# Regrouping wide and narrow matmuls, and one PSUM tile per bank, in the feed-forward part of a decoder layer

## The chip, the core and the metric

The kernel runs on one core of a Trainium2 chip. The metric is the device time in microseconds of one execution, and the number to predict is the median of several runs of the changed kernel. Five engines work side by side, each through its own instruction stream in order: TensorE (PE, with its weight loads as PEld), VectorE (DVE), ScalarE (ACT), GpSimd (POOL, unused here) and SyncE (SP), which issues all loads.

## What is computed

One decoder layer on 256 tokens of width 2048, in float32: two groups of attention heads, an output projection and a gated feed-forward part of inner width 5504. The change lies in the feed-forward part. Cut from the reference:

```python
def conv_ffn(h, w_up, conv_w, conv_b, w_down):
    u = h @ w_up                                   # 2048 -> 2 x 5504
    up = jnp.pad(u, ((0, 0), (CONV_WIDTH - 1, 0), (0, 0)))
    uc = conv_b
    for i in range(CONV_WIDTH):
        uc = uc + up[:, i:i + S] * conv_w[i]
    gate, val = jnp.split(uc, 2, axis=-1)
    return (jax.nn.silu(gate) * val) @ w_down      # 5504 -> 2048
...
h2 = rmsnorm(x, norm2_g[l]) * (1.0 + sc2) + sh2
x = x + g2 * conv_ffn(h2, w_up[l], conv_w[l], conv_b[l], w_down[l])
return rmsnorm(x, final_norm_g)
```

## The kernel before

**Precision.** Every float32 matrix is split into a high part (rounded to the matmul's format) and a low part (the rest): `split` (L142) makes `wh` with a cast on ACT (L145) and `wl` with a subtraction on DVE (L146), 1024 columns at a time, each in a ring of three buffers. A ring slot is refilled when PE has read its last matmul from it. Weights come in loads of 1 MB (2048 columns a partition) into a ring of four `raw` buffers, issued by SP in program order.

**Two ways to multiply.** `trn` (L161) gives three matmuls of 256 columns per 128x128 block of weights: high by high (L163), high by low (L164), low by high (L165). `fold` (L155) gives two: a wide one, `wh` against the 512 columns that hold the high and the low part of the activations side by side (L158), and a narrow one of 256 columns, `wl` against the high part alone (L159). Each matmul loads its own weights. A split of 1024 columns is 8 blocks, called a chunk here: 24 matmuls by `trn`, 16 by `fold`.

**Up projection.** `do_U` (L790) makes the accumulators of one of 43 column tiles f (gate and value) from two loads, i = 0 and 1, and so from four chunks (tiles `wU` f i gv). For f under 8 `trn` is used, and the i = 0 halves of all eight stand ahead of the i = 1 halves, since the second half of the input `h2` is made late; two neighbouring f share one PSUM tile of two banks (tile U0 holds f = 0 and 1). From f = 8 on `fold` is used, and a tile of two banks holds gate and value of one f. After each f its accumulators are drained: for f of 8 and above a copy of the low half on ACT (L836) and an addition on DVE (L837), both 512 wide; then the convolution (L843 on ACT, L847 on DVE), the silu (L849), the product (L853) and the high and low parts of the result (L854, L855) in `aT`.

**Down projection.** The loop at L862 goes through 43 loads of `wD`; 43 blocks make one output tile k, so a chunk of 8 can hold the end of one k and the start of the next. Two neighbouring k share one PSUM tile of two banks (`banks`, L796). When a k is complete, DVE reads it (L875, then L726 in `resid`), ACT squares the result (L731) and scales it (L877).

**What sets the order.** The program is written as one stream; the framework under it works out from the tiles that instructions share which must wait for which, orders each engine's instructions by priority and readiness, and puts in the waits. A PSUM tile is one object to it. Pools give buffers by tag: `s2` (2 KB a partition, four of them) serves the small intermediates of the whole layer: `h` and `g2` of the normalisations, the rotary pieces, the `rl` tiles of the index scores (L549 and on), masks, and `u` and `uc` of the up projection. A table (`PLAN`, L48) and a rate place the `wa` and `wg` loads of the conditioning matrix, with one DVE operation of 2.3 us for each `wa` (L215).

The table of psum pools: stage 3 (up and down) has four buffers of two banks each, eight banks in all.

Of the kernel before, what the change touches and what calls it, by code (L numbers as in the profile page):

```python
# [10 lines left out]
F32 = mybir.dt.float32  # L11
# [3 lines left out]
AF = mybir.ActivationFunctionType  # L15
ALU = mybir.AluOpType
AX = mybir.AxisListType
PSUM = bass.MemoryType.PSUM

P = 128  # L20
D = 2048
S = 256
NT = 2
KT = 16
# [5 lines left out]
FT = 43  # L30
# [8 lines left out]
PB, PN1, PN2, PSG, PDG, PCW, PCB, PC, PGF = 0, 96, 112, 128, 136, 144, 402, 488, 504  # L39
# [15 lines left out]
def layer(ctx: ExitStack, tc: tile.TileContext, a, out):  # L55
    nc = tc.nc
    V, A, T, DMA = nc.vector, nc.scalar, nc.tensor, nc.sync

    cp = ctx.enter_context(tc.tile_pool(name="cp", bufs=1))
    wp = ctx.enter_context(tc.tile_pool(name="wp", bufs=1))  # L60
# [2 lines left out]
        return wp.tile(shape, dt, name=name, tag="b8", bufs=17)  # L63

    def s2(shape, dt, name):
        return wp.tile(shape, dt, name=name, tag="s2", bufs=4)

    def sm(n, name):
        return wp.tile([P, n], F32, name=name, tag="sm", bufs=8)
# [36 lines left out]
    def rb(name):  # L106
        return wp.tile([P, S], F32, name=name, tag="rb", bufs=2)
# [34 lines left out]
    def split(w, off, n, name):  # L142
        wh = wp.tile([P, 1024], F32R, name=name + "h", tag="wh", bufs=3)
        wl = wp.tile([P, 1024], F32R, name=name + "l", tag="wl", bufs=3)
        lo_[1] = A.copy(out=wh[:, 0:n], in_=w[:, off:off + n])  # L145
        lo_[0] = V.tensor_tensor(out=wl[:, 0:n], in0=w[:, off:off + n], in1=wh[:, 0:n].bitcast(F32), op=ALU.subtract)  # L146
        return wh, wl
# [4 lines left out]
        T.matmul(pt, lhsT=xh, rhs=wl, start=False, stop=False)  # L152
        T.matmul(pt, lhsT=xl, rhs=wh, start=False, stop=last)

    def fold(pt, x, wh, wl, first, last):  # L155


        T.matmul(pt, lhsT=wh, rhs=x, start=first, stop=False)  # L158
        T.matmul(pt[:, 1, :], lhsT=wl, rhs=x[:, 0, :], start=False, stop=last)  # L159

    def trn(pt, xh, xl, wh, wl, first, last):  # L161

# [45 lines left out]
    def order(later, earlier):  # L208
        tc.add_manual_dep(later.ins, earlier.ins.name,
                          mybir.DependencyInfo(mybir.DependencyClass.NoSync, mybir.DependencyReason.DATA),  # L210
                          reason="order")
# [512 lines left out]
    def resid(dst, acc, gate, res, sqsum, k, name):  # L724

        resid_i[0] = V.scalar_tensor_tensor(out=dst, in0=acc, scalar=gate, in1=res, op0=ALU.mult, op1=ALU.add)  # L726
        if k == 0:
            A.activation(sqsum, dst, AF.Square)
            return None
        sq = s2([P, S], F32, f"{name}{k}")  # L730
        resid_i[1] = A.activation(sq, dst, AF.Square)  # L731
        if k >= KT - 2:
            return sq
        V.tensor_tensor(out=sqsum, in0=sqsum, in1=sq, op=ALU.add)
# [39 lines left out]


    ctx3 = ExitStack()

    pool3 = ctx3.enter_context(tc.tile_pool(name="psC", bufs=4, space=PSUM))
    psum_pool[0] = (pool3, {"ps": 4})
    ptag[0] = "ps"  # L780

    def banks(name):
        return pool3.tile([P, 2, 2, S], F32, name=name, tag="ps", bufs=4)

    aT = []

    G0 = 8
    uacc = {}

    def do_U(f, i):  # L790

        if i == 0:
            if f >= G0:
                uacc[f] = banks(f"U{f}")
            elif f % 2 == 0:
                t_ = banks(f"U{f}")  # L796
                uacc[f], uacc[f + 1] = t_[:, 0], t_[:, 1]
        w = load(a["wU"][f, i], 2048, f"wU{f}{i}")
        for gv in range(2):
            wh, wl = split(w, gv * 1024, 1024, f"wU{f}{i}{gv}")  # L800
            if (f, i, gv) in ((0, 0, 1), (1, 0, 0)):
                order(lo_[0], resid_i[0])
                if gv == 0:
                    order(lo_[1], resid_i[1])
            for j in range(8):
                k = 8 * i + j
                x = h2[k // 4][:, k % 4, :, :]
                sl = slice(j * P, (j + 1) * P)
                if f >= G0:
                    fold(uacc[f][:, gv], x, wh[:, sl], wl[:, sl], k == 0, k == KT - 1)  # L810
                else:
                    trn(uacc[f][:, gv, :], x[:, 0, :], x[:, 1, :], wh[:, sl], wl[:, sl], k == 0 and gv == 0,
                        k == KT - 1 and gv == 1)

    def eager(n=2):
        for k in range(KT):
# [11 lines left out]
    for f in range(FT):  # L828
        if f >= G0:
            do_U(f, 0)  # L830
        do_U(f, 1)
        acc = uacc.pop(f)
        pump()
        if f >= G0:
            u = s2([P, 2, S], F32, f"u{f}")
            A.copy(out=u, in_=acc[:, :, 1, :])  # L836
            V.tensor_tensor(out=u, in0=acc[:, :, 0, :], in1=u, op=ALU.add)  # L837
        else:
            u = acc
        uc = s2([P, 2, S], F32, f"uc{f}")  # L840
        for gv in range(2):
            i = 2 * f + gv
            A.activation(uc[:, gv, :], u[:, gv, :], AF.Identity, scale=par[:, PCW + 3 * i + 2:PCW + 3 * i + 3],  # L843
                         bias=par[:, PCB + i:PCB + i + 1])
            for sft in (1, 2):
                o = PCW + 3 * i + 2 - sft
                V.scalar_tensor_tensor(out=uc[:, gv, sft:S], in0=u[:, gv, 0:S - sft], scalar=par[:, o:o + 1],  # L847
                                       in1=uc[:, gv, sft:S], op0=ALU.mult, op1=ALU.add)
        last_silu = A.activation(uc[:, 0, :], uc[:, 0, :], AF.Silu)  # L849
        if f % 4 == 0:  # L850
            aT.append(b8([P, 4, 2, S], F32R, f"aT{f}"))
        at = aT[f // 4][:, f % 4, :, :]
        V.tensor_tensor(out=uc[:, 1, :], in0=uc[:, 0, :], in1=uc[:, 1, :], op=ALU.mult)  # L853
        A.copy(out=at[:, 0, :], in_=uc[:, 1, :])  # L854
        V.tensor_tensor(out=at[:, 1, :], in0=uc[:, 1, :], in1=at[:, 0, :].bitcast(F32), op=ALU.subtract)  # L855
# [3 lines left out]
        need(j)  # L859
    V.tensor_tensor(out=mod[:, 80:96], in0=mod[:, 80:96], in1=par[:, PB + 80:PB + 96], op=ALU.add)  # L860
    sq3, last = rb("sq3"), [None, None]
    for q in range(FT):  # L862
        w = load(a["wD"][:, q * 2048:(q + 1) * 2048], 2048, f"wD{q}")
        for p_ in range(2):
            wh, wl = split(w, p_ * 1024, 1024, f"wD{q}{p_}")
            for j in range(8):
                k, f = divmod((2 * q + p_) * 8 + j, FT)
                if f == 0 and k % 2 == 0:
                    acc = banks(f"W{k}")
                fold(acc[:, k % 2], aT[f // 4][:, f % 4, :, :], wh[:, j * P:(j + 1) * P], wl[:, j * P:(j + 1) * P],  # L870
                     f == 0, f == FT - 1)
                if f == FT - 1:
                    xk = x1T[k // 8][:, k % 8, :]
                    g = mod[:, 80 + k:81 + k]
                    V.scalar_tensor_tensor(out=xk, in0=acc[:, k % 2, 0, :], scalar=g, in1=xk, op0=ALU.mult, op1=ALU.add)  # L875
                    last[k % 2] = resid(xk, acc[:, k % 2, 1, :], g, xk, sq3, k, "x2q")
                    A.activation(xk, xk, AF.Copy, scale=par[:, PGF + k:PGF + k + 1])  # L877
    r3 = rms_b([sq3] + last, D, None, "r3", "ps")
    for k, n in ((0, 2), (2, 2), (4, 4), (8, 4), (12, 4)):
        y = x1T[k // 8][:, k % 8:k % 8 + n, :]  # L880
# [72 lines left out]
```

## Time and profile before

| | |
|---|---|
| median of 3 runs | 1251.4 us (1251.29 to 1252.37) |
| the profiled execution's own time | 1258.62 us |
| its span on the core | 1256.8 us |
| PE busy | 1171.3 us (93%) |
| PE weight loads busy | 1016.9 us (81%) |
| DVE busy | 880.5 us (70%) |
| ACT busy | 629.3 us (50%) |
| mean granted TensorE clock | 0.979 |
| DMA | 303.48 MB, mean 241 GB/s |

All times of single instructions come from the one profiled execution. A matmul's recorded duration reaches past the start of the next one, since they are pipelined; what a matmul costs in a stream is therefore read from the distance between starts (its pitch), not from its duration. In the trace's stretches, up runs from about 477 to 988 us (f under 8 until about 595) and down from about 988 to 1243 us.

### The profile page before, as it was taken

How to read it: one execution, taken by the hardware profiler on the slowest of the kernel's cores; microseconds unless marked ns; L12 is line 12 of the kernel's file. 1: busy time of each engine (PE TensorE's matmuls, PEld its weight loads, DVE VectorE, ACT ScalarE, POOL GpSimd, SP SyncE). 2: the span in 40 equal slices, each digit the busy share in tenths (PEclk: the TensorE clock that was granted, in tenths of full speed). 3: DMA queues.
4: the chain of work that ended last, by engine and by line, in shares of the span. 5: the costliest groups of instructions: out<-in, count | busy, mean ns of one | idle time of the engine just before them, and what ended most of it. 6: DMA issues, size and time to landing. Idle time of an engine off the chain costs nothing.

```text
span 1256.8 us, 17813 instructions
## 1 busy us (share of the span) xinstructions
PE 1171.3 (93%) x7120; PEld 1016.9 (81%) x7120; DVE 880.5 (70%) x1232; ACT 629.3 (50%) x969; POOL 0.2 (0%) x4
## 2 busy tenths in 40 slices
PE   4699999899999997988999999999999999999995
PEld 2478987567879997987888888888888888888885
DVE  4877787789667888756789778777777645545443
ACT  3355554466555544454555555555555543443441
POOL 0000000000000000000000000000000000000000
PEclk9799999999999998999999999999999999999998
DMA  8988989667678896844578666666665445455431
GB/s 307 365 332 303 339 331 336 231 252 277 228 293 351 298 330 258 306 165 168 181 250 316 224 226 229 215 241 224 214 225 190 179 172 192 172 175 183 179 135 67
DMA packets 43282, 303.48 MB, mean 241 GB/s; under 512 B 4928, under 2 KB 5440, under 8 KB 7232
## 3 DMA queue, kind: packets, MB, share of 16 engines
q1 hardware_dynamic: 43200, 302.35, 66.0%
q8 instruction: 55, 0.90, 0.3%
q14 instruction: 27, 0.22, 0.0%
HBM read 300.24 MB, written 2.10 MB: 241 GB/s over the span
## 4 chain that ended last, share of the span: by engine, by line
PE 82%; DVE 11%; ACT 3%; DMA 2%; issue 2%; SPq 0%; DVEq 0%; ACTq 0%
PE U L158 20%; PE W L158 13%; PE U L159 10%; PE W L159 6%; DVE wa L215 3%; PE U L165 2%; PE U L164 2%; PE U L163 2%; PE O L165 2%; PE O L163 2%; PE O L164 2%; PE QK L163 2%; PE QK L164 2%; PE QK L165 2%; DMA wa<-wa 2%; PE A L151 2%
## 5 line engine op out<-in xcount | busy, mean ns | idle before, releaser
L215 DVE SCALAR_TENSOR_TENSOR wa<-wa,scb 128x2048 f32<-128x2048 f32 x76 | 173.5, 2285 | 6.9 <-DMA wa<-wa 6.6
L847 DVE SCALAR_TENSOR_TENSOR uc<-u,par,uc 128x254 f32<-128x254 f32 (+1 forms) x140 | 58.2, 478 | 0.0
L843 ACT ACTIVATE uc<-u,par 128x256 f32<-128x256 f32 x70 | 38.2, 593 | 0.8 <-DVE u L837 0.8
L854 ACT CAST aT<-uc 128x256 fp32r<-128x256 f32 x43 | 17.4, 404 | 28.8 <-DVE uc L853 28.7
L313 ACT ACTIVATE amul<-mod,b,par 128x1 f32<-128x1 f32 x32 | 12.0, 385 | 32.2 <-DVE wa L215 32.2
L192 PE MATMUL ap<-wg,csil 128*32 128x512 f32 x160 | 26.4, 679 | 0.3 <-DVE mod L201 0.3
L855 DVE TENSOR_TENSOR aT<-uc,aT 128x256 fp32r<-128x256 f32 x43 | 18.2, 422 | 10.0 <-ACT aT L854 9.9
L837 DVE TENSOR_TENSOR u<-U,u 128x512 f32<-128x512 f32 x35 | 23.9, 684 | 0.0
L316 ACT ACTIVATE mod<-mod,par 128x1 f32<-128x1 f32 x32 | 8.6, 302 | 27.5 <-DVE wa L215 26.6
L836 ACT COPY u<-U 128x512 f32<-128x512 f32 x35 | 20.3, 580 | 0.0
L853 DVE TENSOR_TENSOR uc<-uc 128x256 f32<-128x256 f32 x43 | 18.1, 420 | 1.5 <-ACT uc L849 0.7
L849 ACT ACTIVATE uc<-uc 128x256 f32<-128x256 f32 x43 | 17.7, 411 | 1.5 <-DVE uc L847 1.5
L731 ACT ACTIVATE x2q<-x1T 128x256 f32<-128x256 f32 x15 | 6.2, 415 | 21.3 <-DVE x1T L726 21.2
L875 DVE SCALAR_TENSOR_TENSOR x1T<-W,mod,x1T 128x256 f32<-128x256 f32 x16 | 7.7, 481 | 12.0 <-PE W L159 12.0
L847 DVE SCALAR_TENSOR_TENSOR uc<-U,par,uc 128x255 f32<-128x255 f32 (+1 forms) x32 | 14.5, 477 | 1.4 <-ACT uc L843 1.2
L192 PEld LDWEIGHTS ap<-wg,csil 128*32 128x32 f32 x160 | 4.7, 120 | 10.0 <-issue 8.2
L843 ACT ACTIVATE uc<-U,par 128x256 f32<-128x256 f32 x16 | 9.0, 561 | 7.5 <-DVE uc L847 7.5
L676 ACT ACTIVATE sbt<-sbt 128x384 f32<-128x384 f32 x8 | 4.2, 524 | 14.8 <-DVE sbt L675 14.8
L562 DVE SCALAR_TENSOR_TENSOR scw<-rl,wix,scw 128x128 f32<-128x128 f32 (+1 forms) x28 | 10.4, 409 | 0.0
L545 PE MATMUL rel<-ws,qixT 64*128 64x128 f32 (+1 forms) x64 | 8.5, 345 | 2.0 <-ACT rl L550 2.0
L273 PE MATMUL cb<-ident,csil 128*128 128x128 f32 x16 | 3.6, 422 | 7.1 <-DMA ident<-ident 7.1
L197 ACT COPY rw<-ap 128x512 f32<-128x512 f32 x5 | 2.9, 586 | 14.0 <-PE ap L192 13.3
(2810 smaller groups left out, 4600.7 us busy)
## 6 DMA issues: line engine op xcount, KB each, us to landing
wU<-wU SPq DMA_DIRECT2D x86, 1024.0 KB, 4.8
wa<-wa SPq DMA_DIRECT2D x76, 1024.0 KB, 5.4
wD<-wD SPq DMA_DIRECT2D x43, 1024.0 KB, 4.6
wg<-wg SPq DMA_DIRECT2D x20, 1024.0 KB, 6.2
wA<-wA SPq DMA_DIRECT2D x16, 1024.0 KB, 6.4
wQK<-wQK SPq DMA_DIRECT2D x16, 1024.0 KB, 6.9
wO<-wO SPq DMA_DIRECT2D x16, 1024.0 KB, 6.9
xT<-xT SPq DMA_DIRECT2D x4, 512.0 KB, 5.9
```

What stands on the lines that cost most here:

```text
L151: T.matmul(pt, lhsT=xh, rhs=wh, start=first, stop=False)
L158: T.matmul(pt, lhsT=wh, rhs=x, start=first, stop=False)
L159: T.matmul(pt[:, 1, :], lhsT=wl, rhs=x[:, 0, :], start=False, stop=last)
L163: T.matmul(pt, lhsT=wh, rhs=xh, start=first, stop=False)
L164: T.matmul(pt, lhsT=wh, rhs=xl, start=False, stop=False)
L165: T.matmul(pt, lhsT=wl, rhs=xh, start=False, stop=last)
L192: T.matmul(pt[32 * j:32 * j + 32, :], lhsT=csil[:, k:k + 1].to_broadcast([P, 32]), rhs=w[:, j * 512:(j + 1) * 512], start=q == 0, stop=q == 3)
L215: i = V.scalar_tensor_tensor(out=w, in0=w, scalar=1.0, in1=scb, op0=ALU.mult, op1=ALU.mult, accum_out=mod[:, j:j + 1])
L836: A.copy(out=u, in_=acc[:, :, 1, :])
L837: V.tensor_tensor(out=u, in0=acc[:, :, 0, :], in1=u, op=ALU.add)
L843: A.activation(uc[:, gv, :], u[:, gv, :], AF.Identity, scale=par[:, PCW + 3 * i + 2:PCW + 3 * i + 3], bias=par[:, PCB + i:PCB + i + 1])
L847: V.scalar_tensor_tensor(out=uc[:, gv, sft:S], in0=u[:, gv, 0:S - sft], scalar=par[:, o:o + 1], in1=uc[:, gv, sft:S], op0=ALU.mult, op1=AL ...
```

## The change

Three edits, all in one diff:

1. `fold` takes the eight steps of a chunk and issues the eight wide matmuls first, then the eight narrow ones. Both call sites collect the steps and call it once a chunk.
2. Up and down take one PSUM tile per bank: eight buffers of one bank in place of four of two. In up each f under 8 has a tile of its own, and from f = 8 on gate and value have one each; their drain becomes two copies and two additions of 256 columns in place of one each of 512. In down each k has its own tile, and the reading of a finished k is written behind the whole chunk.
3. The ring `s2` has three buffers in place of four, and `u` moves out of it to a ring `u2` of two.

```diff
     def s2(shape, dt, name):
-        return wp.tile(shape, dt, name=name, tag="s2", bufs=4)
+        return wp.tile(shape, dt, name=name, tag="s2", bufs=3)
...
-    def fold(pt, x, wh, wl, first, last):
-        T.matmul(pt, lhsT=wh, rhs=x, start=first, stop=False)
-        T.matmul(pt[:, 1, :], lhsT=wl, rhs=x[:, 0, :], start=False, stop=last)
+    def fold(steps):
+        for pt, x, wh, _, first, _ in steps:
+            T.matmul(pt, lhsT=wh, rhs=x, start=first, stop=False)
+        for pt, x, _, wl, _, last in steps:
+            T.matmul(pt[:, 1, :], lhsT=wl, rhs=x[:, 0, :], start=False, stop=last)
...
-    pool3 = ctx3.enter_context(tc.tile_pool(name="psC", bufs=4, space=PSUM))
-    psum_pool[0] = (pool3, {"ps": 4})
+    pool3 = ctx3.enter_context(tc.tile_pool(name="psC", bufs=8, space=PSUM))
+    psum_pool[0] = (pool3, {"ps": 8})
...
-    def banks(name):
-        return pool3.tile([P, 2, 2, S], F32, name=name, tag="ps", bufs=4)
+    def bank(name):
+        return pool3.tile([P, 2, S], F32, name=name, tag="ps", bufs=8)
...
         if i == 0:
-            if f >= G0:
-                uacc[f] = banks(f"U{f}")
-            elif f % 2 == 0:
-                t_ = banks(f"U{f}")
-                uacc[f], uacc[f + 1] = t_[:, 0], t_[:, 1]
+            uacc[f] = [bank(f"U{f}{gv}") for gv in range(2)] if f >= G0 else bank(f"U{f}")
...
         if f >= G0:
-            u = s2([P, 2, S], F32, f"u{f}")
-            A.copy(out=u, in_=acc[:, :, 1, :])
-            V.tensor_tensor(out=u, in0=acc[:, :, 0, :], in1=u, op=ALU.add)
+            u = wp.tile([P, 2, S], F32, name=f"u{f}", tag="u2", bufs=2)
+            for gv in range(2):
+                A.copy(out=u[:, gv, :], in_=acc[gv][:, 1, :])
+                V.tensor_tensor(out=u[:, gv, :], in0=acc[gv][:, 0, :], in1=u[:, gv, :], op=ALU.add)
...
+            steps, done = [], None
             for j in range(8):
                 k, f = divmod((2 * q + p_) * 8 + j, FT)
-                if f == 0 and k % 2 == 0:
-                    acc = banks(f"W{k}")
-                fold(acc[:, k % 2], aT[f // 4][:, f % 4, :, :], wh[:, j * P:(j + 1) * P], wl[:, j * P:(j + 1) * P],
-                     f == 0, f == FT - 1)
+                if f == 0:
+                    wacc[k] = bank(f"W{k}")
+                steps.append((wacc[k], aT[f // 4][:, f % 4, :, :], wh[:, j * P:(j + 1) * P], wl[:, j * P:(j + 1) * P],
+                              f == 0, f == FT - 1))
                 if f == FT - 1:
-                    xk = x1T[k // 8][:, k % 8, :]
...
+                    done = k
+            fold(steps)
+            if done is not None:
+                k = done
+                acc = wacc.pop(k)
+                xk = x1T[k // 8][:, k % 8, :]
...
```

The order of instructions changes beyond what the diff says, at three places. In the rows below (those of the changed kernel have its own line numbers) a tile's name carries its buffer number behind an underscore, `x3` is a repetition, and the engines named in brackets are those that the instruction waits for.

**PE, down projection, where k = 0 ends and k = 1 begins (chunk wD21).** Before:

```order
L158 MATMUL W0_8976<-aT40_8765,wD21h_9077 128x512
L159 MATMUL W0_8976<-aT40_8765,wD21l_9078 128x256
L158 MATMUL W0_8976<-aT0_4957,wD21h_9077 128x512 [waits DVE_49]
L159 MATMUL W0_8976<-aT0_4957,wD21l_9078 128x256
L158 MATMUL W0_8976<-aT0_4957,wD21h_9077 128x512
```

With the change:

```order
L160 MATMUL W0_9085<-aT40_8868,wD21h_9186 128x512 [waits DVE_49]
L160 MATMUL W1_9190<-aT0_4961,wD21h_9186 128x512 [waits PE_49]
L160 MATMUL W1_9190<-aT0_4961,wD21h_9186 128x512 x3
L160 MATMUL W1_9190<-aT4_5238,wD21h_9186 128x512
L162 MATMUL W0_9085<-aT40_8868,wD21l_9187 128x256 [waits DVE_49]
L162 MATMUL W0_9085<-aT40_8868,wD21l_9187 128x256 x2
L162 MATMUL W1_9190<-aT0_4961,wD21l_9187 128x256 x4
L162 MATMUL W1_9190<-aT4_5238,wD21l_9187 128x256
```

The first matmul of k = 1 (on aT0) waited for DVE, because it wrote the tile W0 that DVE was to read for k = 0; now it writes a tile W1 of its own and waits for no other engine. The wait for DVE in the first row of the second piece is for the last column tile of aT40, and that in the fifth for wD21l.

**PE, up projection, behind the last chunk of f = 0.** Before:

```order
L163 MATMUL U0_4354<-h23_4301,wU011h_4921 128x256
L164 MATMUL U0_4354<-h23_4301,wU011h_4921 128x256
L165 MATMUL U0_4354<-h23_4301,wU011l_4922 128x256
L163 MATMUL U2_4471<-h22_4300,wU210h_5032 128x256 [waits Activation_49]
L164 MATMUL U2_4471<-h22_4300,wU210h_5032 128x256
L165 MATMUL U2_4471<-h22_4300,wU210l_5033 128x256 [waits DVE_49]
```

With the change:

```order
L166 MATMUL U0_4354<-h23_4301,wU011h_4925 128x256
L167 MATMUL U0_4354<-h23_4301,wU011h_4925 128x256
L168 MATMUL U0_4354<-h23_4301,wU011l_4926 128x256
L166 MATMUL U1_4413<-h22_4300,wU110h_4967 128x256 [waits Activation_49]
L167 MATMUL U1_4413<-h22_4300,wU110h_4967 128x256
L168 MATMUL U1_4413<-h22_4300,wU110l_4968 128x256 [waits DVE_49]
```

Before, the chunks ran wU011, wU210, wU110, wU111, wU211, wU410, wU310, wU311, wU411, wU610, wU510, wU511, wU611, wU800, wU710, wU711: an even f pushed ahead of the odd one that shares a tile with the f being drained. Now they run in rising order, wU011, wU110, wU111, wU210 and on. ACT and DVE make the splits in rising order in both kernels. At the start of up, the first chunks of f = 0 and f = 1 (wU000 and wU100) are now interleaved, where wU000 and wU001 ran through before wU100.

**DVE, index scores of the sparse attention.** `scw` are the score sums and the top-64 search (m815 to m817 its late steps), `rl` the rectified products, V1040l a split of the value projection that PE uses as a filler. Before:

```order
L568 MAX m815_2038<-scw_131 128x8 [waits DVE_49]
L295 TENSOR_TENSOR qx1v_2068<-qds_196,scw_131 128x8x16
L569 MATCH_REPLACE scw_131<-m815_2038,scw_131 128x256 [waits DVE_49]
L296 TENSOR_TENSOR qds_196<-qx1u_2067,qx1v_2068 128x8x32 [waits DVE_49]
L568 MAX m816_2041<-scw_131 128x8 [waits DVE_49]
L146 TENSOR_TENSOR V1040l_2340<-V10w4_2331,V1040h_2339 128x1024 [waits DMAHW0_49]
```

With the change:

```order
L565 SCALAR_TENSOR_TENSOR scw_131<-rl001_1911,wix_1861,scw_131 128x128 [waits DVE_49]
L565 SCALAR_TENSOR_TENSOR scw_131<-rl010_1927,wix_1861,scw_131 128x128 [waits DVE_49,Activation_49]
L146 TENSOR_TENSOR V1040l_2340<-V10w4_2331,V1040h_2339 128x1024 [waits DMAHW0_49]
L565 SCALAR_TENSOR_TENSOR scw_131<-rl010_1927,wix_1861,scw_131 128x128 [waits DVE_49]
L565 SCALAR_TENSOR_TENSOR scw_131<-rl011_1933,wix_1861,scw_131 128x128 [waits Activation_49]
```

V1040l moved from the end of the search to the first group of scores, and with it the other splits of the value and query-key projections come earlier on ACT and DVE. PE then has V1040 and V1042 matmuls ahead of the transposes kdsp and qdsp, and takes the sparse attention's and the stick-breaking heads' own matmuls somewhat later among the same fillers. SP's order of loads is the same in both kernels.

## Rows read from the trace of the kernel before

**Rows 1.** The page, busy time, share of the span and instructions of engines

```profile
PE 1171.3 (93%) x7120; PEld 1016.9 (81%) x7120; DVE 880.5 (70%) x1232; ACT 629.3 (50%) x969; POOL 0.2 (0%) x4
```

**Rows 2.** Busy by stretch: us, PE, PEld, DVE, ACT, POOL, clock, DMA share, GB/s

```profile
225.00:400.00 175.00, 160.93 (x1062) 128.25 (x1055) 133.73 (x256) 102.14 (x218) 0.00 (x0) 0.98 0.73 271
536.00:600.00 64.00, 54.50 (x391) 51.56 (x391) 41.04 (x65) 31.79 (x49) 0.00 (x0) 0.95 0.46 162
600.00:1000.00 400.00, 399.73 (x2263) 346.30 (x2263) 306.73 (x422) 223.97 (x319) 0.00 (x0) 1.00 0.63 225
1000.00:1245.00 245.00, 232.19 (x1316) 200.64 (x1314) 116.95 (x125) 97.18 (x111) 0.00 (x0) 1.00 0.45 159
```

**Rows 3.** PE's waits: for whom, us in total, times, longest us

```profile
PE W L158 <- DVE x1T L726: 11.5, 8, 2.2
...
PE kdsp L581 <- DVE ws L296: 2.8, 1, 2.8
...
PE U L165 <- DVE wU610l L146: 2.5, 1, 2.5
...
PE U L164 <- DVE h L304: 2.1, 1, 2.1
...
PE U L163 <- ACT wU410h L145: 1.0, 1, 1.0
...
PE U L165 <- DVE wU410l L146: 0.8, 1, 0.8
...
PE U L163 <- DVE uc L847: 0.7, 1, 0.7
```

**Rows 4.** Timeline, PE and DVE, where k = 1 begins: start us, us

```profile
1003.38 0.28 PE L159 MATMUL W<-aT,wD21l 128*128 128x256 f32 x1
...
1005.85 0.51 PE L158 MATMUL W<-aT,wD21h 128*128 128x512 f32 x1 [2.19 <-DVE x1T L726]
...
1004.80 0.48 DVE L875 SCALAR_TENSOR_TENSOR x1T<-W,mod,x1T 128x256 f32<-128x256 f32 x1
```

**Rows 5.** Timeline, PE, folds of up and of down until k = 0

```profile
688.68 0.40 PE L158 MATMUL U<-h,wU1610h 128*128 128x512 f32 x1
688.92 0.28 PE L159 MATMUL U<-h,wU1610l 128*128 128x256 f32 x1
...
999.61 0.40 PE L158 MATMUL W<-aT,wD20h 128*128 128x512 f32 x1
```

**Rows 6.** Timeline, PE, folds of down in k = 5 and 6, second and last

```profile
1069.23 0.40 PE L158 MATMUL W<-aT,wD131h 128*128 128x512 f32 x1
...
1098.35 0.40 PE L158 MATMUL W<-aT,wD181h 128*128 128x512 f32 x1
```

**Rows 7.** Timeline, PE, ends of an all-512 and an all-256 stretch

```profile
102.37 0.39 PE L151 MATMUL V<-V0000h,hh 128*128 128x512 f32 x1
...
123.91 0.39 PE L153 MATMUL V<-V0142h,hl 128*128 128x512 f32 x1
124.14 0.28 PE L163 MATMUL QK<-hh,wQK0000h 128*128 128x256 f32 x1
...
170.09 0.28 PE L165 MATMUL QK<-hh,wQK0710l 128*128 128x256 f32 x1
```

**Rows 8.** Timeline, ACT, DVE and PE, where chunk wU210 comes out of turn

```profile
537.10 1.04 ACT L145 CAST wU210h<-wU 128x1024 fp32r<-128x1024 f32 x1 [1.83 <-PE U L164]
...
538.18 1.23 DVE L146 TENSOR_TENSOR wU210l<-wU,wU210h 128x1024 fp32r<-128x1024 f32 x1 [1.65 <-ACT wU210h L145]
...
538.20 0.39 PE L163 MATMUL U<-h,wU210h 128*128 128x256 f32 x1 [1.02 <-ACT wU210h L145]
```

**Rows 9.** Busy by stretch, behind the wait for wU410l; columns as in rows 2

```profile
553.30:557.30 4.00, 4.00 (x23) 4.00 (x24) 3.44 (x9) 1.33 (x4) 0.00 (x0) 0.65 0.30 127
```

**Rows 10.** Timeline, DVE, the split V1040l

```profile
257.41 1.21 DVE L146 TENSOR_TENSOR V1040l<-V10w,V1040h 128x1024 fp32r<-128x1024 f32 x1
```

**Rows 11.** The page, a DVE group: busy us, mean ns, idle before

```profile
L837 DVE TENSOR_TENSOR u<-U,u 128x512 f32<-128x512 f32 x35 | 23.9, 684 | 0.0
```

More of the change, by code (lines that the diff above doesn't have):

```diff
@@ L804, in do_U @@
                     order(lo_[1], resid_i[1])
+            steps = []
             for j in range(8):
@@ L809, in do_U @@
                 if f >= G0:
-                    fold(uacc[f][:, gv], x, wh[:, sl], wl[:, sl], k == 0, k == KT - 1)
+                    steps.append((uacc[f][gv], x, wh[:, sl], wl[:, sl], k == 0, k == KT - 1))
                 else:
@@ L861, in layer @@
     sq3, last = rb("sq3"), [None, None]
+    wacc = {}
     for q in range(FT):
@@ L865, in layer @@
             wh, wl = split(w, p_ * 1024, 1024, f"wD{q}{p_}")
+            steps, done = [], None
             for j in range(8):
                 k, f = divmod((2 * q + p_) * 8 + j, FT)
-                if f == 0 and k % 2 == 0:
-                    acc = banks(f"W{k}")
-                fold(acc[:, k % 2], aT[f // 4][:, f % 4, :, :], wh[:, j * P:(j + 1) * P], wl[:, j * P:(j + 1) * P],
-                     f == 0, f == FT - 1)
+                if f == 0:
+                    wacc[k] = bank(f"W{k}")
+                steps.append((wacc[k], aT[f // 4][:, f % 4, :, :], wh[:, j * P:(j + 1) * P], wl[:, j * P:(j + 1) * P],
+                              f == 0, f == FT - 1))
                 if f == FT - 1:
-                    xk = x1T[k // 8][:, k % 8, :]
[L874 to L877, printed above, removed]
+                    done = k
+            fold(steps)
+            if done is not None:
+                k = done
+                acc = wacc.pop(k)
+                xk = x1T[k // 8][:, k % 8, :]
+                g = mod[:, 80 + k:81 + k]
+                V.scalar_tensor_tensor(out=xk, in0=acc[:, 0, :], scalar=g, in1=xk, op0=ALU.mult, op1=ALU.add)
+                last[k % 2] = resid(xk, acc[:, 1, :], g, xk, sq3, k, "x2q")
+                A.activation(xk, xk, AF.Copy, scale=par[:, PGF + k:PGF + k + 1])
     r3 = rms_b([sq3] + last, D, None, "r3", "ps")
```

## Prediction

> **What bounds the kernel now.** I read the page first, then the busy time by stretch, PE's list of waits, and the timeline of PE where the waits fall. On the page PE is busy for 93% of the span and no other engine for more than 70% [rows 1]. An average hides stages, so the second view matters more [rows 2]: from 600 to 1000 us, the up projection with folds, PE is busy for 399.73 of 400 us at a clock of 1.00. There nothing but PE's own pace can be worth time. From 1000 to 1245 (down) PE stands idle for 245 - 232.2 = 12.8 us, from 536 to 600 (the i = 1 halves of f under 8) for 9.5, and from 225 to 400 (the attention) for 14.1. The list of waits names them: in down all eight are one kind, a wide matmul that waits for DVE's L726, 11.5 us together; between 536 and 600 they are waits for splits [rows 3].
>
> **PE's pace.** A pair of fold takes 0.3533 us in up: from 688.68 to 999.61 us there are 880 pairs [rows 5]. In k = 5 and 6 of down the same pairs take 0.3467: 84 between the two rows [rows 6]. Down has both paces; each holds from one wait to the next: k = 3 to 6 and 9, 10 (258 pairs) run at the faster one, the other 430 at the slower. Streams of one width take 0.2267 us a matmul at 512 columns (95 steps) and 0.1200 at 256 columns (383 steps) [rows 7]. Their sum, 0.3467, is the faster pace. In the slower one the wide matmul takes 0.24 to the start of its narrow one [rows 5], so the excess sits at the change from wide to narrow.
>
> **The change, part by part**, against the profiled execution's own 1258.6 us:
>
> *1. A tile of its own for each k in down.* The first matmul of every odd k waits until DVE has read the k before it, because both lie in one tile; DVE was busy with another split until 1004.80 and only then read it [rows 4]. With the change that matmul waits for no other engine. What it costs is more than the listed idle time: from 1003.38 to 1005.85 are 2.47 us where 0.12 is the pitch, so 2.35 is lost for a listed 2.19, and the late matmul itself takes 0.51 for 0.40 [rows 4]; 0.16 + 0.10 come on top of each wait. Removed: 11.5 + 8 x 0.26 = 13.6 us. What is late next? DVE's two readings of k, 0.48 each [rows 4], and ACT's steps on it stand ahead of the splits of a later chunk; but the ring of three holds two chunks (5.5 us) in reserve, and DVE is busy for only 117 of 245 us, ACT for 97 [rows 2]. I expect nothing of it on the path. Bounds: 10 to 13.6.
>
> *2. A tile of its own for each f under 8.* The shared tile made the builder push an even f ahead of the odd one. The splits come in rising order into a ring of three, so the chunk taken out of turn is the fourth: its cast can only start when PE has finished the chunk before it (537.10), PE gets it at 538.20, and DVE's part later still [rows 8]. PE pays cast and subtraction in full, 1.0 + 0.8 us, at wU210, wU410 and wU800, and 1.0 + 2.5 at wU610, where a `wa` operation stood in DVE's way; one more of 0.7 waits for the drain [rows 3]. That is 9.6 us in nine waits, with the same 0.26 each 11.9. [...] Together 14.7. In rising order the ring is two chunks (5.8 us) ahead. DVE is busy there for 41 us, 75% of the 54.5 in which PE works [rows 2], and once holds a `wa` as well, so I leave 1.2 us for one late split and take 13.5. Bounds: 6 (half comes back) to 14.7.
>
> *3. f = 0 and f = 1 interleaved.* PE waits 2.1 us for a late piece of `h2`, while DVE does a `wa` [rows 3]. With wU100's matmuls between, PE has work in that time. I take 2, bounds 0 to 4.
>
> *4. Eight wide, then eight narrow.* All 1120 pairs of up and 430 of down run at 0.3533; at the sum of the one-width pitches [rows 7] each saves 6.6 ns: 1550 x 0.0066 = 10.3 us. A chunk keeps one change from wide to narrow and one back. If these keep the excess, 226 chunks give back 226 x 6.6 ns = 1.5 us; nothing shows it, so I take half: 9.5. Bounds 0 and 10.3. In the same edit `wh` is free 0.96 us earlier and `wl` needed 1.8 us later, which only adds slack.
>
> *5. Drains in halves.* 35 additions of 684 ns [rows 11] become 70; the nearest row for 256 columns out of PSUM is 0.48 us [rows 4], so DVE has up to 35 x 0.276 = 9.7 us more, ACT about as much. Both are covered: DVE is busy for 307 of the 400 us there, ACT for 224 [rows 2]. Without that cover it would be up to 10 us. I take 0.
>
> *6. `s2` with three buffers.* It moves work in the attention part, where 14.1 us of PE idle time lie. V1040l, at 257.41 before [rows 10], now stands among the first scores, some 20 us earlier; so PE has 48 matmuls of 0.2267 (10.9 us) to fill what were waits for kdsp (2.8 [rows 3]) and its neighbour qdsp (1.2). Against this, DVE's top-k search, which that stretch hangs on, starts 2.4 us later for two splits, and with three `rl` buffers ACT is less far ahead. Later the heads have fewer fillers left. PE's total work is the same, so the price is the change of those 14.1 us. I take a gain of 3, bounds -6 and +8. In the first 225 us only a few steps of `h` change places on DVE and ACT; I take 0.
>
> **Sum:** 13.6 + 13.5 + 2 + 9.5 + 0 + 3 = 41.6. 1258.6 - 41.6 = 1217.0 in the profiled execution, which ran 7.2 us above the median; taken off the median of 1251.4 it is 1209.8, say **1210 us**. The bounds of parts 1 to 4 and 6 would add up to 1201 and 1241; they are independent, so about 1203 to 1217 for this case alone.
>
> **Rivals.**
>
> *A. The order within a chunk is worth nothing* (chance 0.13). The two paces of down were seen with the same alternating order, so the excess may be a state into which the stream falls after a wait, whatever the order. For it: each pace holds from wait to wait. Against it: neither of the two one-width streams [rows 7] shows a second pace. Then part 4 is 0: 1219.5. [...]
>
> *B. The bubbles of part 2 come back in another place* (0.09): DVE, busy for 75% of PE's time in that stretch [rows 2], falls behind the ring of three at each f, and PE waits about 1.2 us eight times: 1210 + 9.6 = 1220.
>
> *C. The attention part gets worse* (0.10): the fillers are used up early, and the stick-breaking heads, each a chain ACT, DVE, PE, leave PE idle. At the bound of part 6 that is 9 us more than forecast: 1219. A mix of A, B and C would be near 1228.
>
> *D. Slower than before* (0.03). In up with folds, the drain is now four steps that pass between ACT and DVE for each f, ahead of casts in ACT's queue. If they hold the refill of the ring up beyond its two chunks, PE pays cast and subtraction at every f as it did at wU210: 1.8 + 0.26 = 2.1 us x 35 = 72 us, 1251.4 - 41.6 + 72 = 1282. It decides from 1.2 us a f (41.6 / 35) upwards. For it: DVE is busy for 77% [rows 2]. Against it: DVE's queue still has a quarter free there, and ACT, busy for 56%, has long idle times in which it waits for PE to free a slot, as the 1.83 us ahead of wU210h [rows 8].
>
> *E. The waits of down stay* (0.02), since DVE or ACT holds up something else there: 1223. The order of the changed kernel shows no wait for DVE at that matmul, so I give this little.
>
> **How the numbers follow.** The forecast's case has 0.63. A range from 1202 to 1226 holds it with its bounds and A, B, C and E; outside are D, mixes of rivals and a gain beyond the bounds, some 0.15. A measurement of this kernel tells 0.2% (2.5 us) from no change; all cases but D, and a sliver of mixes, are far beyond that: faster 0.96, same 0.01, slower 0.03.
>
> **What would show it.** In the profile after: no wait of PE for L726's successor in down, and about 30 us from every second k to the next; no waits for wU210, wU410, wU610, wU800 and no clock under 1.00 between 536 and 590; 16 matmuls of a fold chunk in 2.77 us (2.78 with the seams) instead of 2.83; kdsp without its 2.8 us. The prediction is wrong if chunks still take 2.83, if PE shows waits for `wU` splits in up beyond a few us in all, or if 225 to 400 lasts longer than 175 us.

## The result and the profile after

The changed kernel takes **1209.0 us** (median of 4 runs, 1206.1 to 1209.1); the kernel before, run beside it, 1251.4 (4 runs, 1249.2 to 1252.4). The ratio is 0.966, 95% interval 0.964 to 0.968. The forecast was 1210.0. The profiled execution took 1209.0 us with a span of 1207.2; that of before had a span of 1256.8. So the traces differ by 49.6 us and the medians by 42.3, and these 7 us will matter below.

The page of the changed kernel, busy time as in [rows 1]:

```profile
PE 1154.3 (96%) x7120; PEld 1015.3 (84%) x7120; DVE 886.8 (73%) x1267; ACT 630.6 (52%) x1004; POOL 0.2 (0%) x4
```

PE works 17 us less for the same 7120 matmuls, and its idle time went from 85.5 us to 52.9. The busy time by stretch (columns as in [rows 2]) shows where; the last three are the i = 1 halves of f under 8, up with folds, and down:

```profile
225.00:400.00 175.00, 169.96 (x1146) 139.75 (x1145) 142.16 (x261) 107.01 (x224) 0.00 (x0) 0.97 0.76 284
516.00:568.00 52.00, 52.00 (x421) 51.33 (x420) 42.19 (x66) 32.27 (x51) 0.00 (x0) 1.00 0.63 222
568.00:953.00 385.00, 385.00 (x2206) 338.76 (x2206) 306.62 (x446) 219.91 (x346) 0.00 (x0) 1.00 0.64 230
953.00:1195.00 242.00, 241.16 (x1385) 212.25 (x1384) 123.93 (x136) 104.06 (x121) 0.00 (x0) 1.00 0.47 170
```

From the start of the i = 1 halves to the last matmul of down, at 1193.5 us, PE has no idle time and a clock of 1.00; the 0.8 us missing in the last row lie behind it. PE's waits, in the order of [rows 3]:

```profile
PE A L151 <- ACT hh L311: 9.7, 2, 8.5
PE cb L276 <- DMA ident<-ident: 7.6, 1, 7.6
PE A L151 <- ACT wA10h L145: 6.2, 1, 6.2
...
PE U L166 <- ACT h L306: 1.9, 1, 1.9
```

What is left lies mostly at the kernel's start, with some 4 us in the attention and 1.9 us ahead of the first matmul of up, which before had too. The waits of W, of wU210 to wU800, of `h` (L304, 2.1 us) and of kdsp are gone; in a second trace of the changed kernel, below, kdsp waits 1.2 us. Between the same matmuls in both traces, this is where the 49.6 us went:

| stretch | before | after | gain | forecast |
|---|---|---|---|---|
| start to the first index-score transposes (kixp) | 228.8 | 227.1 | 1.7 | 0 |
| kixp to the first matmul of O (the attention) | 145.6 | 135.9 | **9.7** | 3 |
| O, to wU000 | 104.5 | 104.7 | -0.2 | 0 |
| start of up, wU000 to wU010 | 52.3 | 48.6 | 3.7 | 2 |
| i = 1 halves of f under 8, to wU810 | 66.4 | 51.7 | 14.8 | 13.5 |
| folds of up, wU810 to wD00 | 390.6 | 385.5 | 5.1 | 9.5 with down |
| down, to its last matmul | 255.0 | 240.1 | 14.9 | 13.6 |
| tail | 13.6 | 13.7 | -0.1 | 0 |

The folds, in the timeline of PE (start, us, from where one width begins to where the next does):

```profile
567.95 0.40 PE L160 MATMUL U<-h,wU810h 128*128 128x512 f32 x1
...
704.82 2.00 PE L160 MATMUL U<-h,wU2011h 128*128 128x512 f32 x8
706.66 1.11 PE L162 MATMUL U<-h,wU2011l 128*128 128x256 f32 x8
707.61 2.00 PE L160 MATMUL U<-h,wU2100h 128*128 128x512 f32 x8
...
953.43 0.40 PE L160 MATMUL W<-aT,wD00h 128*128 128x512 f32 x1
```

Eight wide take 1.84 us, eight narrow 0.95, a chunk 2.79: 138 chunks in 385.48 us, 2.793 each, and every chunk from wU810 to the end of down is within 0.01 us of it. In rows of one width they would take 2.774 [rows 7]. Averaged over 111 chunks, the first five wide matmuls after narrow ones take 6.6, 9.2, 1.6, 5.8 and 4.2 ns more than 226.7, the first two narrow ones 6.7 and 0.9 less than 120.0: 20 ns a chunk.

The drains in halves, DVE and ACT (busy us, mean ns, idle before), for [rows 11]:

```profile
L838 DVE TENSOR_TENSOR u<-U,u 128x256 f32<-128x256 f32 x70 | 29.2, 417 | 0.7 <-ACT u L837 0.7
L837 ACT COPY u<-U 128x256 f32<-128x256 f32 x70 | 25.3, 362 | 0.0
```

DVE pays 5.3 us more for 70 additions than for the 35 before, beside a PE that never waits.

### The profile page after: what moved, and what is told of

Read it like the earlier page. It is cut to its first block, busy times and chain, and to the rows that moved or that the text cites. A ratio compares the mean times of both kernels' runs of the same rounds, so it can differ in the third digit from the quotient of the medians.

```text
span 1207.2 us, 17866 instructions
## 1 busy us (share of the span) xinstructions
PE 1154.3 (96%) x7120; PEld 1015.3 (84%) x7120; DVE 886.8 (73%) x1267; ACT 630.6 (52%) x1004; POOL 0.2 (0%) x4
## 4 chain that ended last, share of the span: by engine, by line
PE 88%; DVE 5%; ACT 3%; DMA 2%; issue 1%; SPq 0%; DVEq 0%; ACTq 0%
PE U L160 21%; PE W L160 13%; PE U L162 11%; PE W L162 7%; PE U L166 3%; PE U L167 3%; PE U L168 3%; PE O L166 3%; PE O L168 3%; PE O L167 3%; PE QK L166 2%; PE QK L167 2%; PE QK L168 2%; DVE wa L218 2%; PE ap L195 1%
## 5 line engine op out<-in xcount | busy, mean ns | idle before, releaser
L848 DVE SCALAR_TENSOR_TENSOR uc<-u,par,uc 128x255 f32<-128x255 f32 (+1 forms) x140 | 66.4, 480 | 17.6 <-ACT uc L844 15.7
L844 ACT ACTIVATE uc<-u,par 128x256 f32<-128x256 f32 x70 | 42.0, 600 | 40.3 <-DVE u L838 40.3
L838 DVE TENSOR_TENSOR u<-U,u 128x256 f32<-128x256 f32 x70 | 29.2, 417 | 0.7 <-ACT u L837 0.7
L837 ACT COPY u<-U 128x256 f32<-128x256 f32 x70 | 25.3, 362 | 0.0
L195 PE MATMUL ap<-wg,csil 128*32 128x512 f32 x160 | 23.4, 640 | 0.6 <-DMA wg<-wg 0.3
L855 ACT CAST aT<-uc 128x256 fp32r<-128x256 f32 x43 | 17.4, 404 | 3.1 <-DVE uc L854 3.1
L151 PE MATMUL A<-wA00h,hh 128*128 128x512 f32 x4 | 2.5, 669 | 8.5 <-ACT hh L311 8.5
L729 DVE SCALAR_TENSOR_TENSOR x1T<-O,mod,xT 128x256 f32<-128x256 f32 x16 | 7.0, 478 | 4.2 <-PE O L168 4.2
```

What stands on the lines that cost most here:

```text
L195: T.matmul(pt[32 * j:32 * j + 32, :], lhsT=csil[:, k:k + 1].to_broadcast([P, 32]), rhs=w[:, j * 512:(j + 1) * 512], start=q == 0, stop=q == 3)
L837: A.copy(out=u[:, gv, :], in_=acc[gv][:, 1, :])
L838: V.tensor_tensor(out=u[:, gv, :], in0=acc[gv][:, 0, :], in1=u[:, gv, :], op=ALU.add)
```

## Experiments

Theory: the six parts as forecast. Rivals: the order within a chunk is worth nothing (A), or the gains are given back elsewhere. Four kernels make one part alone on the kernel before or undo a group of parts; the others follow what these showed. In all, before was run more than 50 times beside them: 1246.5 to 1262.5 us. The groups ran on different chips, on which the median of before was 1251.0 to 1255.6, so a distance to the changed kernel's 1209.0 is only good to a few us, and the traces' stretches are given beside it.

**Part 1 alone.** In down, a two-bank tile for each k:

```
-                if f == 0 and k % 2 == 0:
+                if f == 0:
                     acc = banks(f"W{k}")
-                fold(acc[:, k % 2], ...
+                fold(acc[:, 0], ...
...
```

> The kernel before with part 1 alone (a two-bank tile for each k of down, of which one half is used). Theory: the eight waits for L726 vanish, each listed wait plus 0.26 us, 13.6 us in all, so 1237.8 us against 1251.4; down takes some 241.5 us where it took 255. Rival E (another wait takes their place, since DVE's two readings still stand ahead of later splits): 1249 to 1251, and PE's list shows new waits in down. Rival 2 (the two paces of down depend on these waits): all 430 pairs fall to the slow pace of 0.3533, which takes 1.7 us back from the pairs that now run at 0.3467: 1239.5.

Measured: 1238.7 us, ratio 0.988 (0.984 to 0.992), which is 16.1 below the 1254.9 of before beside it where 13.6 was forecast; the interval holds both. There is no wait in down. But its six runs are of two kinds: 1233.0, 1234.0, 1234.4 (the first three) and 1243.1, 1243.5, 1243.6 (the last three). The trace belongs to one of the first; from wU1601 on, PE in its timeline:

```profile
682.93 0.39 PE L158 MATMUL U<-h,wU1601h 128*128 128x512 f32 x1
...
979.68 0.39 PE L158 MATMUL W<-aT,wD00h 128*128 128x512 f32 x1
```

107 chunks in 296.75 us are 2.773 each, 0.3467 a pair: the alternating stream of **up**, which took 0.3533 in before [rows 5], runs at the faster pace here, with the same instructions in the same order. It keeps it through down, 192 chunks. Ahead of it one chunk, wU1600, is longer (2.88 us), and up to there the pace was the slower one. At the slower pace 192 chunks take 192 x 0.053 = 10.2 us more; the two kinds of runs are 9.5 apart. That the upper three ran at the slower pace fits, but only the profiled one has a trace, and as they came in a row, something else that lasted is not excluded by this run alone. In the trace all of down ran at the faster pace, so some 2.9 of the 16.6 us by which down is shorter than in before (238.4 for 255.0) are pace; the expectation that it would all fall to the slower one did not hold there.

**Part 4 alone.** The new `fold` on the old tiles, drain of k after its chunk:

> The kernel before with part 4 alone: eight wide matmuls, then their eight narrow ones, on the old tiles. Theory of the prediction: 9.5 us, 1241.9. By the chunks of the changed kernel (2.793 us where 2.831 stood, 140 chunks in up, and in down 54 of the slow ones gained and 32 of the fast ones made 0.02 us longer): 140 x 0.037 + 54 x 0.037 - 32 x 0.019 = 6.6 us, 1244.8. Rival A (order is worth nothing): 1251.4.

Measured: 1260.7 us, ratio 1.005 (1.003 to 1.007): **slower** than before, as no theory had it. The chunks of up take 2.793, as expected. Down takes 267.4 us where it took 255.0. PE's list of waits, and the timeline of PE and DVE at k = 1:

```profile
PE W L160 <- DVE x1T L729: 17.4, 8, 2.2
```

```profile
995.47 0.48 DVE L888 SCALAR_TENSOR_TENSOR x1T<-W,mod,x1T 128x256 f32<-128x256 f32 x1 [1.39 <-PE W L162]
995.87 1.22 DVE L146 TENSOR_TENSOR wD40l<-wD,wD40h 128x1024 fp32r<-128x1024 f32 x1
997.00 0.48 DVE L729 SCALAR_TENSOR_TENSOR x1T<-W,mod,x1T 128x256 f32<-128x256 f32 x1
...
997.63 3.03 PE L160 MATMUL W<-aT,wD30h 128*128 128x512 f32 x8 [2.20 <-DVE x1T L729]
...
1000.45 1.77 PE L162 MATMUL W<-aT,wD30l 128*128 128x256 f32 x8
```

The narrow matmul that ends k now comes at the end of the chunk, so both of DVE's readings and the split between them lie in front of the next chunk: 2.2 us, eight times (11.5 us in all before [rows 3]). And behind five of the eight the granted clock falls; the busy time of one such stretch (columns as in [rows 2], clock 0.53):

```profile
998.30:1001.30 3.00, 3.00 (x11) 2.48 (x10) 0.00 (x0) 0.78 (x2) 0.00 (x0) 0.53 0.02 5
```

The eight wide of wD30 take 2.82 us (997.63 to 1000.45) where 1.84 are usual. Against the down of the changed kernel (240.1), the eight chunks that end in the waits cost 18.8 us more and the five at the lower clock 8.2 more. Behind the waits, once the clock is back, the chunks take 2.793 again. So grouping loses on the tiles of before; it pays, by the run below that undoes it, where each k has a tile of its own.

**Part 6 alone**, on before; `u` moves to its own pool of two, as in the change:

```
-        return wp.tile(shape, dt, name=name, tag="s2", bufs=4)
+        return wp.tile(shape, dt, name=name, tag="s2", bufs=3)
```

> The kernel before with part 6 alone: three buffers of s2, and the drains of up in a pool of two of their own. Forecast: 3 us, 1248.4. By the two profiled executions, in which the stretch from the first index scores to the first matmul of O took 145.6 us before and 135.9 in the changed kernel: 9.8 us, 1241.6. Rival (most of those 9.8 us belong to that one execution of before, which ran 7.2 above its median): 9.8 - 7.2 = 2.6 us, 1248.8, and a trace in which the stretch takes about 136 us all the same. Rival C (worse): above 1253.

Measured: 1244.2 us, ratio 0.993 (0.9905 to 0.9955): 10.6 us below the median of 1254.9 of before beside it, 8.8 by the ratio. From kixp to O, busy time by stretch of the first experiment (whose attention is that of before), and of this one:

```profile
227.60:371.50 143.90, 134.37 (x849) 104.76 (x849) 111.25 (x219) 86.86 (x192) 0.00 (x0) 0.96 0.69 251
```

```profile
227.70:363.00 135.30, 130.31 (x839) 103.35 (x839) 110.83 (x219) 85.07 (x187) 0.00 (x0) 0.99 0.75 273
```

Of 8.6 us, 4.5 are idle time (9.5 to 5.0); the stretch holds ten matmuls fewer, and the one behind it, to the sum of the heads' normalisation (rsbp), takes 1.3 us more (10.2 for 8.9); the other 2.8 are put to the clock, 0.99 for 0.96, as what is left over. Between the traces of before and of the changed kernel the split is another:

```profile
228.80:374.40 145.60, 133.61 (x848) 104.84 (x848) 111.05 (x219) 86.76 (x192) 0.00 (x0) 0.98 0.69 248
```

```profile
227.10:363.00 135.90, 131.73 (x840) 104.36 (x840) 111.05 (x219) 85.30 (x187) 0.00 (x0) 0.96 0.73 271
```

There 7.8 of 9.7 us are idle time (12.0 to 4.2), and the clock is lower after than before, so it is no part of that gain. Beside kdsp and qdsp, these waits of before are gone from the trace after, for splits of the query-key projection and in the stick-breaking heads:

```profile
PE u L672 <- DVE sbt L670: 2.6, 2, 2.3
...
PE QK L163 <- ACT wQK1300h L145: 1.3, 1, 1.3
...
PE QK L165 <- DVE wQK1200l L146: 1.2, 1, 1.2
```

The rival, that the gain belonged to one execution, has fallen by the medians, and by the other traces: with three buffers of `s2` the stretch took 132.6 to 136.0 us in eight traces, with four or six 143.4 to 145.6 in five. The folds of up took 385.2 us in this trace, again mostly at the faster pace.

**Parts 2, 3 and 5 undone** in the changed kernel:

```
-            uacc[f] = [bank(f"U{f}{gv}") for gv in range(2)] if f >= G0 else bank(f"U{f}")
+            if f >= G0:
+                uacc[f] = banks(f"U{f}")
+            elif f % 2 == 0:
+                t_ = banks(f"U{f}")
+                uacc[f], uacc[f + 1] = t_[:, 0], t_[:, 1]
...
```

> The changed kernel with parts 2, 3 and 5 undone: two-bank tiles, f under 8 shared by two, drains whole; down keeps a tile for each k, and grouping and buffers stay. Theory by the traces: the i = 1 halves get their 14.8 us back and the start of up 3.7, so 1209.0 + 18.5 = 1227.5; the forecast's terms give 13.5 + 2 = 15.5, 1224.5. Rival (the shared tile cost only what the listed waits say, 9.6 + 2.1 us, and no clock): 1220.7. Rival (the drains in halves cost as much as they were allowed, up to 10 us of DVE on the path, so whole drains win it back): 1217.5 or less.

Measured: 1226.1 us, ratio 0.978 (0.975 to 0.980), 17.1 above the changed kernel (13.6 when each is taken from the before beside it: 28.7 and 42.3). The waits are back:

```profile
PE U L168 <- DVE wU610l L146: 2.3, 1, 2.3
...
PE U L166 <- ACT wU410h L145: 1.0, 1, 1.0
...
PE U L168 <- DVE wU410l L146: 0.8, 1, 0.8
```

and so is the lower clock, in the busy time of the i = 1 halves; the second row holds the folds of up:

```profile
515.90:581.50 65.60, 56.94 (x418) 54.44 (x417) 41.00 (x62) 31.62 (x47) 0.00 (x0) 0.95 0.50 179
581.50:967.00 385.50, 385.50 (x2211) 339.26 (x2210) 300.44 (x413) 219.44 (x313) 0.00 (x0) 1.00 0.65 229
```

Against the changed kernel the i = 1 halves cost 14.0 us more and the start of up 2.2, together 16.2. The folds take 385.48 us in both, with whole drains and with halves: part 5 is worth 0.

**Part 4 undone** in the changed kernel:

```
-        for pt, x, wh, _, first, _ in steps:
+        for pt, x, wh, wl, first, last in steps:
             T.matmul(pt, lhsT=wh, rhs=x, start=first, stop=False)
-        for pt, x, _, wl, _, last in steps:
             T.matmul(pt[:, 1, :], lhsT=wl, rhs=x[:, 0, :], start=False, stop=last)
```

> The changed kernel with part 4 undone: wide and narrow matmuls alternate again, all else stays. Theory: 140 chunks of up go from 2.793 back to 2.831 us, 5.2 us; down's 86 chunks have no waits left that could start the slow pace or end it, so they lie between all slow (3.2 us more) and all fast (1.7 less): 1212.5 to 1217.4. The forecast's 9.5 would give 1218.5. Rival A (order is worth nothing): 1209.0.

Measured: 1216.8 us, ratio 0.972 (0.969 to 0.975): five runs from 1216.3 to 1219.1 and one of 1208.4. The traced one ran at the slower pace from the first folds to the end of down; a part of it:

```profile
658.47 0.40 PE L160 MATMUL U<-h,wU1610h 128*128 128x512 f32 x1
...
958.10 0.40 PE L160 MATMUL W<-aT,wD00h 128*128 128x512 f32 x1
```

106 chunks in 299.63 us are 2.827 each. So the alternating stream showed two paces, 2.773 and 2.827 a chunk, and in all traces kept one until a wait or a longer chunk; the same code was traced at either. The stream in groups of eight showed, away from waits, 2.793 and no other in seven traces. That the one run of 1208.4 met the faster pace is likely, but it has no trace.

**Part 6 undone** in the changed kernel, four buffers that `u` shares:

> The changed kernel with part 6 undone: four buffers of s2, which the drains of up share again. By the two profiled executions 9.8 us: 1218.8. Forecast 3 us: 1212.0. Rival (7.2 of the 9.8 belonged to one execution of before): 1211.6. In each case the difference lies between the first index scores and the first matmul of O, where kdsp waits for DVE again (2.8 us), and up takes as long as in the changed kernel.

Measured: 1216.4 us (1215.9 to 1218.4), ratio 0.972 (0.971 to 0.974), 7.4 above the changed kernel. Kixp to O takes 143.4 us and PE waits 2.8 for kdsp; folds and down take what they did.

**Two, and six, buffers** in the changed kernel, to see whether the number or the order counts:

> The changed kernel with two buffers of s2 where it has three. Theory (with fewer buffers the score steps on DVE wait for the next one, the split of V1040 goes ahead of them, and PE has V's matmuls to fill what were waits for kdsp and its neighbours): V1040l stands ahead of all score steps here, ten places earlier than with three, so the stretch from the index scores to the first matmul of O takes 134 to 137 us again, 1206 to 1210. Rival (ACT is now one relu ahead instead of two, so DVE waits for each rl and the top-k search starts late): 3 to 8 us more, 1212 to 1217, all of it in that stretch. In up and down nothing changes.

> The changed kernel with six buffers of s2. Theory (what counts is where the scheduler puts V1040l, not the number of buffers as such): V1040l stands after the score steps, as with four, so the stretch from the index scores to the first matmul of O takes some 143 us and the kernel 1216 to 1218, as with four (1216.4). Rival (with four the buffers were short, and more of them help): 1209 or less.

Measured: two, 1220.0 us, ratio 0.971 (0.969 to 0.974); six, 1217.9, ratio 0.969 (0.966 to 0.972). Six behaves as four: 144.7 us from kixp to O, 4.5 of it a wait for kdsp. Two loses, though V1040l stands earliest in the order (in time it starts at 235.6 us, 235.7 in the changed kernel): 138.8 us there, and outside, where neither theory nor rival had anything, PE waits for the first products of up's input, which also live in `s2` (1.9 us in the changed kernel), and for kixp:

```profile
PE U L166 <- DVE g L305: 4.9, 1, 4.9
...
PE kixp L519 <- ACT kd L518: 2.1, 1, 2.1
```

So the theory that only the place of V1040l counts falls: of two, three, four and six, three is best, between fillers that come late and buffers that are short.

**Groups of sixteen**, and **of four**, wide and narrow:

> The changed kernel with sixteen wide matmuls in a row and then their sixteen narrow ones (both halves of a loaded weight) in up from f = 8 and in down. In the trace the first five wide matmuls after a change from narrow take 27 ns more in all than the others, the first two narrow ones 8 ns less: 20 ns a change. With 113 changes fewer: 2.2 us, 1206.8. Rival (the ring of three, of which a group now holds two, runs dry): PE waits for a split in each group, 1 to 2 us in up to 113 groups, far above 1209. Rival (the excess goes with the number of wide matmuls, not of changes): 1209.0.

> The changed kernel in groups of four wide and four narrow matmuls. In the changed kernel the first four wide ones after narrow ones take 6.6, 9.2, 1.6 and 5.8 ns more than 226.7, the first two narrow ones 6.7 and 0.9 less than 120.0: 15.6 ns a group of four, 31 a chunk, against 20 now: 226 x 11 ns = 2.6 us, 1211.6, in every run alike. Rival (a group of four is already an alternating stream with two paces): runs of two kinds, between 1204.6 and 1216.7. Rival A (order is worth nothing): 1209.0.

Measured: sixteen, 1208.2 us, ratio 0.965 (0.963 to 0.967); down takes 0.86 us less from its first matmul to r3p (the last normalisation's sum), 43 x 20 ns, up 0.44 less, with a wait of 0.7 in it. The run cannot be told from the changed kernel's. Four, 1210.8 us, ratio 0.966 (0.963 to 0.969), in one kind of runs; the folds of up take 387.35, 2.807 a chunk for the 2.805 expected:

```profile
566.50 0.40 PE L161 MATMUL U<-h,wU810h 128*128 128x512 f32 x1
...
953.85 0.40 PE L161 MATMUL W<-aT,wD00h 128*128 128x512 f32 x1
```

**Alternating, with the narrow ones a chunk late**, to hold the faster pace:

```
+        old = lag[:]
+        for i in range(max(len(steps), len(old))):
...
+                T.matmul(pt, lhsT=wh, rhs=x, start=first, stop=False)
...
+                T.matmul(pt[:, 1, :], lhsT=wl, rhs=x[:, 0, :], start=False, stop=last)
+        lag[:] = steps
```

> The changed kernel with wide and narrow alternating all through, the narrow ones a chunk late: eight wide of the first chunk, then in turn a wide of chunk c + 1 and a narrow of chunk c, to the end of down; drains a chunk later. The traces so far: an alternating stream runs at 0.3467 or 0.3533 us a pair, and changes only at a wait; eight wide in a row end without any excess. Theory 1 (after eight wide without excess the alternating stream keeps the faster pace): 226 chunks of 2.774 for 2.793 us, 4.4 us less, 1204.6. Theory 2 (the pace is drawn by chance at each wait, and this start changes nothing): runs of two kinds, 1204.6 and 226 x 2.827 us, 7.7 more, 1216.7. Rival (each change from narrow to wide costs, so all runs are slow): 1216.7 in every run.

> The changed kernel as it is, beside the two others on one chip: 1206 to 1209, as in its four runs so far. If the grouped stream has one pace only, all chunks between the start of the folds and the last matmul take 2.793 us again, and the runs spread by no more than 3 us; if it has two as well, some runs lie 7 us or more above or 4 below.

Measured: lagged 1216.1 us, ratio 0.970 (0.966 to 0.973), one run of 1205.3 and five from 1215.0 to 1219.0: as theory 2 has it, with one trace. That trace runs at the slower pace, although eight wide matmuls stand ahead of it. The changed kernel beside it: 1208.2 us, ratio 0.964 (0.962 to 0.967), 1206.2 to 1210.0, every chunk 2.793; the spread of 3.8 is above the 3 expected, with no run 7 above or 4 below. No version here beats it by more than the runs spread.

## Why the prediction was right, and where its steps were not

*Part 1 (13.6):* right. The eight chunks of before that held the wait took 36.2 us for 8 x 2.80: 13.8. Made alone it changed what it should, and no wait took its place. But the prediction calls the parts independent, and parts 1 and 4 are not: without part 1, part 4 made the waits longer (17.4 us for 11.5) and the kernel 5.9 us slower. The prediction looked at what the new order does to `wh` and `wl`, and not at a finished k, which now ends with its chunk and is read later.

*Part 2 (13.5) and 3 (2):* part 2 right; part 3 low, inside its bounds. 14.8 and 3.7 in the traces of before and after, 14.0 and 2.2 in that of the run that undid them, whose median is 13.6 to 17.1 above. The 3.7 are the wait of 2.1 that part 3 names and, behind it, a stretch at a clock of 0.50 in before (486.3 to 489.7 us) that the sum did not count. In the i = 1 halves PE meets no wait for a split and no clock under 1.00, so the 1.2 us left for one late split was not needed. The 14.7 from which these were taken are the 11.9 of the waits and 2.8 for the two stretches of 4 us in which before shows a clock of 0.65, from 553.3 [rows 9] and from 570.4: 2 x 4 x 0.35, an estimate from those clocks.

*Part 4 (9.5):* the step that failed is "all 1120 pairs of up and 430 of down run at 0.3533", taken as what before costs. That was what one execution cost. The same code ran the folds of up in 384.4 us in one trace and 390.6 in another. Grouping takes 7.7 us off an alternating run at the slower pace (226 x 0.034) and adds 4.5 to one at the faster (226 x 0.020); undone, it cost 7.8 by medians, where five of six runs lay at 1216 and above. The seams, bounded at 6.6 ns, cost 20. Nor does the excess sit at the change from wide to narrow, as the prediction read it: in the grouped stream it is in the first five wide matmuls after narrow ones, which alternating rows could not tell apart. *Rival A* had the mechanism, a pace that a stream falls into at a wait; it was wrong that order does nothing, since only the alternating order showed the two; the streams of one width, each matmul with its own weights, took 226.7 ns at 512 columns and 120.0 at 256 [rows 7].

*Part 5 (0):* right, and not only argued: 385.48 us with and without it. *Rival D* has fallen with it.

*Part 6 (3):* the term that was mis-sized, 7.4 to 10.6 by medians. I took the two listed waits that V1040 would fill (4.0) and set a delay of the search against them. The idle time fell by 4.5 in one pair of traces, about the first, and by 7.8 in another: besides those two waits, the ones of QK (2.5) and u (2.6) went, which the sum did not have, and of the delay no net cost shows. The 1.3 us of work that moved out of the stretch are no gain of the kernel. *Rival C* went the other way.

*The sum:* 41.6 was set against the profiled 1258.6, 1217.0, and 49.6 came. Then 7.2 was taken off since that execution ran above the median. Of these 7.2, the slower pace throughout up would account for 6.2 (390.6 for 384.4) if the runs at the median had the faster one, of which there is no trace; the changed kernel, which showed no such pace to draw, profiled at its median. So that the total came out within 1 us is luck: a gain of 8.0 more than the sum in the traces (6.7 of it part 6) met a correction of 7.2 that did not carry over to the changed kernel. The range was right on better grounds, since it had room for the bounds and for A to C. *Rivals B* and *E* did not come: no wait for a split in the i = 1 halves, none in down.

## What to carry to other kernels

A tile that two accumulations share ties PE to the reader of the first and can reorder the work; give each its own tile before changing the order of matmuls, since grouping alone made the wait longer here. Compare a stream's pace between runs, not only within one: a term that rests on the pace of one execution may not hold in the next. Vary a buffer count both ways and read every stage that uses the tag; here fewer was better from four to three, worse from three to two.

## What the runs showed of the hardware that was not expected

- Alternating matmuls of 512 and 256 columns ran at 0.3467 or 0.3533 us a pair, up to 192 chunks without change; what sets the pace at a wait stays open. Eight wide ones ahead of the stream did not bring the faster one in the one trace of it.
- After narrow matmuls, five wide ones passed before the pitch was 226.7 ns again: 20 ns net a change back and forth at eight and at sixteen in a row. In groups of four it was 17 (2.807 us a chunk for 2.774, two changes).
- With part 4 alone the granted clock fell behind the waits of 2.2 us in down in five of eight cases (0.53 over the 3 us from 998.3, 0.52 over the 3 us from 1032.5); behind the waits of before, listed with 11.5 us in all, it stayed at 1.00 [rows 2]. In the run with part 6 alone, whose down is that of before, it fell behind one of the eight, a wait of 2.2 us (0.57 from 990.5 to 994.5 us). What decides it stays open.
